# Issuing a kernel's DRAM stores from ScalarE instead of SyncE

## The chip, the cores and the metric

One core of a Trainium2 chip runs the program. The metric is the device time of one execution in microseconds (us). SP is the engine SyncE, which here does nothing but issue transfers; ACT is ScalarE, DVE VectorE, POOL GpSimd, PE TensorE.

## The reference

A one-layer hybrid encoder step, for a prompt of 2048 positions with 16 learned positions ahead of it, and for 8 short streams of 16 positions that have 256 cached positions each. All is float32.

```python
h = rmsnorm(x, norm_g)
q, k, v, z_a, f, B, C, h_c, z_c = split(h @ w_in)          # w_in: 1024 x 4104
logf = log_sigmoid(f + b_f);  c = cumsum(logf)              # per head
s = q.k / 8 + c_q - c_k, causal                             # 8 heads of 64
o = softmax(s) @ v * silu(z_a)
u = C * h_c;  y = B * conv3(u) * silu(z_c)                  # causal, width 3
x = x + concat(o, y) @ w_out
return rmsnorm(x, final_g), k, v, logf, last rows of u      # prompt and streams
```

## The kernel before

Float32 products are made of three float32r products: each operand is split into a high part (a ScalarE cast) and a low part (a VectorE subtraction), hence names that end in `h` and `l`.

The work comes in two token groups (1280 positions, then the rest). For each group the tokens are normalised and transposed (`hh`, `hl`), then the projections run: `keys`, `queries`, `gates` and `values` for four pairs of heads, later `conv` for four blocks of channels. Each projection fetches 128 columns of `w_in` (`raw`, 512 KB, issued from ScalarE), splits them (`wh`, `wl`) and runs 24 products into a PSUM tile `ps`, of which there are two. ScalarE or VectorE takes the result out into `kf`, `eh`, `el`, `sv`, `vv` or `st`, and it is stored to DRAM: keys to `kh_d` and `kl_d`, queries to `qh_d` and `ql_d`, gates to `gz_d`, values to `v_d`, convolution results to `cat_d`; outputs of the reference go to `out_dram`. `eh` and `el` have one buffer each (`EB = 1`), `kf` and `st` have two or fewer, so the next tile of that name waits until the store has landed.

Attention takes these back from DRAM: per head `ka`, `kb` and `vb`, per unit of 256 queries `qa`, `qb` and `gz`, and the running sums `c_d` in rows of 1 KB. A unit makes scores (`sp`, `s`), an exponential on ScalarE, transposes (`tp`), the split `ph` (ScalarE) and `pl` (VectorE), products with `vb` into `o`, and a store of the gated result to `cat_d`. Attention and projections are woven on TensorE. At the end the output stage loads 128 columns of positions from `cat_d` (`cr`), splits them (`ch`, `cl`), multiplies by `w_out`, adds `x`, normalises (`oxt`) and stores `y`, tile by tile.

The order of the work is fixed when the program is built. `Times` keeps a running clock for each engine; `weave` picks the next TensorE work by it, and every instruction of the other engines, transfers too, gets a key from the same clock, by which `settle` sorts each engine's queue. All engines but TensorE then go through their queue in that order. A transfer is an entry in the queue of the engine that issues it: it waits there for its data, for the room it writes to, and for one of eight completion counters (DMAHW0 to DMAHW7 in the program), which go round over the transfers of all queues; what stands behind it waits too.

Before the change every transfer but the 59 loads of `raw` goes through `Step.dma`:

```python
    def dma(self, out, in_):
        ...
        return self.nc.sync.dma_start(out=out, in_=in_)
```

Of the kernel before, what the change touches and what calls it, by code (L numbers as in the profile page):

```python
# [18 lines left out]
DRAM = bass.MemoryType.DRAM  # L19
# [48 lines left out]
class Times:  # L68
# [85 lines left out]
    def note(self, queue, op, a, k):  # L154
        k = dict(k)
        if op == "matmul":
            k.update(zip(("out", "lhsT", "rhs"), a))
        elif a:
            k.update(zip(("out", "in_"), a))
        writes = [k[x] for x in ("out", "accum_out") if k.get(x) is not None]  # L160
        if not writes:
            return
        reads = [self.region(v) for x, v in k.items() if isinstance(v, bass.AP) and x not in ("out", "accum_out")]
        cost_of, writes = writes[0], [self.region(w) for w in writes]
        ready = max(self.free(reads, False, queue), self.free(writes, True, queue))
        if op == "dma_start":
            size, run = 4.0, min(4.0 * self.run(k["out"]), 4.0 * self.run(k["in_"]))
            for x in cost_of.shape:
                size *= x
            size = max(size * (2 if run < 512 else 1) / 360.0, 0.4375 * size / run)  # L170
            self.key = self.place(queue, ready, 50.0) + self.LATENCY
            t = self.place("dge", self.key - self.LATENCY, 450.0 if cost_of.shape[0] == P else 650.0)
            t = self.place("dma", t + DMA_START, size)
            if queue == "sync":
                self.key = t - size
            t += DMA_LATENCY
        else:
            t = self.place(queue, ready, self.cost(queue, op, cost_of, k)) + self.LATENCY
            self.key = t
        for regions, wrote in ((reads, False), (writes, True)):  # L180
            for name, lo, hi in regions:
                if wrote and name not in self.begun:
                    self.begun[name] = t
                old = self.seen.setdefault(name, [])
                if len(old) > 100:
                    old[:] = [x for x in old if x[2] > self.pe - 40000.0]
                old.append((lo, hi, t, wrote, queue))
                self.used[name] = max(self.used.get(name, 0.0), t)
        return t
# [125 lines left out]
class Step:  # L315
# [7 lines left out]
    def dma(self, out, in_):  # L323

        if out.dtype == F32R:
            out = out.bitcast(F32)
        if in_.dtype == F32R:
            in_ = in_.bitcast(F32)
        return self.nc.sync.dma_start(out=out, in_=in_)

    def open(self, ctx, name, side=None, space=None):
        k = {}
# [47 lines left out]
    def load_constants(self, pool):  # L380
        nc, dma = self.nc, self.dma
        mraw = pool.tile([P, P], F32, name="mraw")
        dma(out=mraw, in_=self.cst[:, C_MASK:C_MASK + P])
        nc.vector.tensor_copy(out=self.mask, in_=mraw)
        for i in range(3):
            dma(out=self.cw[:, :, i], in_=self.conv_w[0, i].rearrange("(c p) -> p c", p=P))

        nc.vector.tensor_scalar(out=self.cw, in0=self.cw, scalar1=0.5, scalar2=None, op0=ALU.mult)
# [22 lines left out]
    def normalise(self, ph, xp, bufs, beside=()):  # L411
# [7 lines left out]
        def prepare():  # L419
            i, (pos, rows, ct, col) = todo.pop(0)  # L420
            xt = xp.tile([P, D], F32, name="xt", bufs=bufs)
            if pos == 0:
                dma(out=xt[:NMETA], in_=self.meta_tokens)
                dma(out=xt[NMETA:], in_=self.x_p[:P - NMETA])
            else:
                dma(out=xt[:rows], in_=self.x_s if pos == NPOS else self.x_p[pos - NMETA:pos - NMETA + rows])
            if pos == p0:
                dma(out=g_bc, in_=self.norm_g[0].partition_broadcast(P))
            if beside:
                beside.pop(0)()  # L430
            sq = xp.tile([P, D], BF16, name="sq")
            ss = xp.tile([P, 1], F32, name="ss", bufs=4)
            nc.scalar.activation(out=sq[:rows], in_=xt[:rows], func=AF.Square, accum_out=ss[:rows])
            self.rsqrt(ss[:rows])
            nc.vector.scalar_tensor_tensor(out=xt[:rows], in0=xt[:rows], scalar=ss[:rows, 0:1], in1=g_bc[:rows],
                                           op0=ALU.mult, op1=ALU.mult)
            ahead.append((xt, rows, ct, col, i))
# [834 lines left out]
    def load_out(self, pool, chunks, freed=()):  # L1272
# [3 lines left out]
        for c, n in chunks:  # L1276
# [8 lines left out]
            for a in range(2):  # L1285
                self.dma(out=self.o_hl[c, n][a], in_=self.o_d[a, :, c, cols])
            if c % PACE == PACE - 1:
                yield self.when(*self.o_hl[c, n])
# [256 lines left out]
WEARLY = 5  # L1545
EARLY = lambda e, a, b: [lambda: None, lambda: (e(a), e(b))]
PACE = 2
HI_ACT = 4
KFB = 2
GTN = 2  # L1550
# [69 lines left out]
```

## Time and profile before

| | us |
|---|---|
| three runs | 1741.93, 1729.77, 1734.06 |
| median | 1734.06 |
| the profiled execution | 1732.57 |
| its span, first to last instruction | 1730.8 |
| TensorE busy in it | 1578.8 |
| VectorE busy | 881.1 |
| ScalarE busy | 629.2 |
| GpSimd busy | 232.9 |

The rows quoted further down are from that one execution; times in them count from its first instruction. Busy time leaves out the issuing of transfers. All rows carry line L278, the helper that records every instruction, so that groups are told apart by tile.

### The profile page before, as it was taken

To read this page: it belongs to the slowest core of one execution; us is meant where nothing else is said; L and a number is where in the kernel's file an instruction comes from. 1 tells how busy PE (TensorE), PEld (TensorE's weight loads), DVE (VectorE), ACT (ScalarE), POOL (GpSimd) and SP (SyncE) were. 2 spreads that over 40 slices of the span, in tenths; PEclk is the share of its full clock that TensorE was granted. 3 is DMA by queue.
4 is the path that set the end of the run, shared out by engine and by line. 5 is a ranking of instruction groups with operands and counts; after the bars stand their busy time and mean duration, and the time that the engine had idled before them with its cause. 6 is when DMAs were issued, how large, how long until landed. Compare 5 with 4: busy or idle time off the path is not lost.

```text
span 1730.8 us, 27628 instructions
## 1 busy us (share of the span) xinstructions
PE 1578.8 (91%) x10311; PEld 1462.5 (84%) x10311; DVE 881.1 (51%) x2276; ACT 629.2 (36%) x1196; POOL 232.9 (13%) x320
## 2 busy tenths in 40 slices
PE   4977899989889899989995789999999999979998
PEld 4877889989889888989984779989889889968876
DVE  4424566526657566624321547667667657313443
ACT  4323445415435242421110435445545445312111
POOL 2200112100001120121020001000110101112222
PEclk9988999989999999999997889999999999989999
DMA  6454544364542386432136444446533413254443
GB/s 165 161 138 107 136 111 120 99 162 112 138 104 65 108 287 216 131 94 50 42 80 130 110 108 118 120 101 160 129 77 76 104 41 72 64 191 158 130 125 122
DMA packets 222241, 206.03 MB, mean 119 GB/s; under 512 B 26036, under 2 KB 196060, under 8 KB 220444
## 3 DMA queue, kind: packets, MB, share of 16 engines
q1 hardware_dynamic: 160748, 173.34, 34.0%
q10 hardware_dynamic: 61360, 30.94, 10.2%
q8 instruction: 81, 1.33, 0.3%
q14 instruction: 52, 0.43, 0.1%
HBM read 137.28 MB, written 66.93 MB: 118 GB/s over the span
## 4 chain that ended last, share of the span: by engine, by line
PE 59%; DMA 22%; DVE 5%; SPq 4%; issue 3%; ACT 3%; POOL 2%; ACTq 0%; POOLq 0%; DVEq 0%
PE ps L278 33%; PE sp L278 9%; PE o L278 9%; PE tp L278 7%; DMA raw<-in_w_in_dram 4%; SPq L278 4%; DMA cr<-cat_d 4%; DVE oxt L278 2%; DMA vb<-v_d 2%; PE tr L278 2%; DMA qh_d<-eh 1%; DMA qb<-ql_d 1%; DMA kb<-kh_d 1%; DMA gz_d<-kf 1%; DMA sqk_d<-el 1%
## 5 line engine op out<-in xcount | busy, mean ns | idle before, releaser
L278 PE MATMUL ps<-hh,wh 128*128 128x256 f32 (+2 forms) x1568 | 502.7, 321 | 23.6 <-DVE el L278 22.8
L278 PE MATMUL ps<-hl,wh 128*128 128x256 f32 (+2 forms) x1568 | 486.3, 310 | 0.0
L278 PE MATMUL ps<-hh,wl 128*128 128x256 f32 (+2 forms) x1568 | 486.0, 310 | 0.0
L278 PEld LDWEIGHTS ps<-hh,wh 128*128 128x128 f32 x1568 | 302.8, 193 | 34.1 <-DVE el L278 23.9
L278 PEld LDWEIGHTS ps<-hl,wh 128*128 128x128 f32 x1568 | 302.5, 193 | 1.8
L278 PEld LDWEIGHTS ps<-hh,wl 128*128 128x128 f32 x1568 | 301.5, 192 | 0.0
L278 DVE TENSOR_TENSOR pl<-tp,ph 128x512 fp32r<-128x512 f32 (+2 forms) x360 | 199.3, 564 | 121.3 <-ACT ph L278 117.7
L278 ACT CAST ph<-tp 128x512 fp32r<-128x512 f32 (+2 forms) x360 | 171.7, 486 | 224.4 <-PE tp L278 204.6
L278 DVE TENSOR_SCALAR_CACHE_REDUCE s<-sp 128x384 f32<-128x384 f32 (+3 forms) x360 | 211.4, 598 | 50.4 <-PE sp L278 48.8
L278 ACT ACTIVATE s<-s,nm 128x128 f32<-128x128 f32 (+16 forms) x136 | 170.5, 1254 | 84.4 <-DVE nm L278 81.9
L278 PE MATMUL tp<-ident,s 128*128 128x128 f32 (+1 forms) x1224 | 196.4, 272 | 5.0 <-DVE pl L278 5.0
L278 PE MATMUL o<-ph,vb 128*128 128x256 f32 (+4 forms) x584 | 169.8, 310 | 16.5 <-DMA vb<-v_d 11.4
L278 PEld LDWEIGHTS tp<-ident,s 128*128 128x128 f32 (+1 forms) x1224 | 148.5, 142 | 29.1 <-issue 20.9
L278 PE MATMUL sp<-kb,qb 68*128 68x384 f32 (+3 forms) x360 | 144.7, 402 | 24.2 <-DMA qb<-ql_d 20.5
L278 PE MATMUL o<-pl,vb 128*128 128x256 f32 (+4 forms) x584 | 151.2, 285 | 2.0 <-DVE pl L278 1.9
L278 POOL TENSOR_TENSOR gz<-gz,otmp 64x256 f32<-64x256 f32 (+1 forms) x64 | 47.1, 737 | 702.2 <-DVE otmp L278 629.5
L278 PE MATMUL sp<-ka,qa 128*128 128x384 f32 (+3 forms) x360 | 133.7, 371 | 0.0
L278 PEld LDWEIGHTS o<-ph,vb 128*128 128x128 f32 (+1 forms) x584 | 111.7, 191 | 23.9 <-DMA vb<-v_d 12.0
L278 PE MATMUL ps<-o,ch 128*128 128x512 f32 x374 | 118.9, 399 | 11.1 <-ACT ch L278 8.9
L278 PEld LDWEIGHTS o<-pl,vb 128*128 128x128 f32 (+1 forms) x584 | 112.4, 192 | 3.3 <-DVE pl L278 2.6
L278 PEld LDWEIGHTS ps<-o,ch 128*128 128x128 f32 x374 | 70.6, 191 | 29.7 <-ACT ch L278 9.3
L278 DVE TENSOR_TENSOR wl<-raw,wh 128x1024 fp32r<-128x1024 f32 x56 | 69.3, 1238 | 47.5 <-ACT wh L278 47.3
(193 smaller groups left out, 2080.5 us busy)
## 6 DMA issues: line engine op xcount, KB each, us to landing
raw<-in_w_in_dram ACTq DMA_DIRECT2D x59, 512.0 KB
cr<-cat_d SPq DMA_DIRECT2D x17, 512.0 KB
v_d<-vv SPq DMA_DIRECT2D x32, 256.0 KB
vb<-v_d SPq DMA_DIRECT2D x8, 1024.0 KB
oxt<-in_x_prompt_dram SPq DMA_DIRECT2D x16, 512.0 KB
out_dram<-oxt SPq DMA_DIRECT2D x16, 512.0 KB
xt<-in_x_prompt_dram SPq DMA_DIRECT2D x15, 512.0 KB
qa<-qh_d SPq DMA_DIRECT2D x112, 64.0 KB
```

What stands on the lines that cost most here:

```text
L278: r = f(*a, **k)
```

## The change

`Step.dma` picks the engine by where the transfer writes: to DRAM, ScalarE; else SP as before. The loads of `raw` were on ScalarE already. In `Times` the price of an issue by GpSimd is changed as well, but no transfer is issued from there.

```diff
-            self.key = self.place(queue, ready, 50.0) + self.LATENCY
+            self.key = self.place(queue, ready, 1000.0 if queue == "gpsimd" else 50.0) + self.LATENCY
...
-        return self.nc.sync.dma_start(out=out, in_=in_)
+        return getattr(self.nc, STORES if out.space == DRAM else "sync").dma_start(out=out, in_=in_)
...
+STORES = "scalar"
```

The built program has 1129 transfers, of which 422 write to DRAM. The order of the other engines moves a little too, since the clock that sorts them sees other queues.

ScalarE's queue before, where the second token group's last queries and first gates are projected (`eh`: high part of the queries, `kf`: gates, `wh<-raw`: weight split; in brackets what a row waits for, PE and DVE for their results, DMAHW for a completion counter):

```order
L278 ACTIVATE eh<-ps 128x272 [waits DMAHW2_49,PE_49]
L278 ACTIVATE kf<-ps 128x256 [waits PE_49] x2
L278 CAST wh<-raw 128x1024 [waits DMAHW5_49,PE_49]
L278 DMA raw<-in_w_in_dram 128x8x128 [waits DMAHW4_49,DVE_49]
L278 ACTIVATE kf<-ps 128x272 [waits DMAHW6_49,PE_49]
```

The same place of ScalarE's queue after the change:

```order
L278 ACTIVATE eh<-ps 128x272 [waits DMAHW7_49,PE_49]
L278 DMA qh_d_92<-eh 128x272 [waits Activation_49]
L278 DMA raw<-in_w_in_dram 128x8x128 [waits DMAHW1_49,DVE_49]
L278 ACTIVATE kf<-ps 128x256 [waits PE_49]
L278 DMA ql_d_96<-el 128x272 [waits DMAHW3_49,DVE_49]
L278 DMA gz_d_111<-kf 128x256 [waits DMAHW5_49,DVE_49]
L278 ACTIVATE kf<-ps 128x256 [waits PE_49]
L278 CAST wh<-raw 128x1024 [waits DMAHW1_49,PE_49]
L278 DMA raw<-in_w_in_dram 128x8x128 [waits DMAHW3_49,DVE_49]
L278 DMA gz_d_111<-kf 128x256 [waits DMAHW4_49]
```

Four stores now stand between the evacuations of `ps`, each with waits of its own.

SP's queue before, at the same place (`ka` and `kb`: keys of a head, `qa` and `qb`: queries of a unit):

```order
L278 DMA ka_9632<-kh_d_100 64x2064
L278 DMA qh_d_92<-eh 128x256
L278 DMA ql_d_96<-el 128x256
L278 DMA ka_9632<-kl_d_104 64x2064
L278 DMA qh_d_92<-eh 128x272
L278 DMA ql_d_96<-el 128x272
L278 DMA kb_9634<-kh_d_100 64x2064
L278 DMA ka_9633<-kh_d_100 64x2064
L278 DMA ka_9633<-kl_d_104 64x2064
L278 DMA kb_9635<-kh_d_100 64x2064
L278 DMA qa_9637<-qh_d_92 64x256 x2
```

SP's queue there after the change:

```order
L278 DMA ka_9632<-kh_d_100 64x2064
L278 DMA ka_9632<-kl_d_104 64x2064
L278 DMA kb_9634<-kh_d_100 64x2064
L278 DMA ka_9633<-kh_d_100 64x2064
L278 DMA ka_9633<-kl_d_104 64x2064
L278 DMA kb_9635<-kh_d_100 64x2064
L278 DMA qa_9637<-qh_d_92 64x256 x2
L278 DMA qb_9639<-ql_d_96 64x256
```

The stores between the loads are gone, and the six loads of two heads follow each other.

## Rows read from the trace of the kernel before

**Rows 1.** The page: busy time, share of the span and instructions.

```profile
PE 1578.8 (91%) x10311; PEld 1462.5 (84%) x10311; DVE 881.1 (51%) x2276; ACT 629.2 (36%) x1196; POOL 232.9 (13%) x320
```

**Rows 2.** Stretches of the span; columns in the first row.

```profile
core 0: us, PE busy (x) PEld busy (x) DVE busy (x) ACT busy (x) POOL busy (x), PEclk, DMA share, GB/s
...
890.00:1030.00 140.00, 100.93 (x695) 93.41 (x694) 52.63 (x137) 42.27 (x78) 12.74 (x10) 0.85 0.54 117
1030.00:1260.00 230.00, 229.57 (x1650) 209.10 (x1650) 151.84 (x430) 117.37 (x215) 19.30 (x28) 0.99 0.47 121
...
1560.00:1705.00 145.00, 142.94 (x615) 114.78 (x614) 57.49 (x50) 26.21 (x37) 37.68 (x25) 1.00 0.44 141
```

**Rows 3.** TensorE's waits: us in total, times, longest us.

```profile
PE ps L278 <- DVE el L278: 22.8, 4, 10.1
PE sp L278 <- DMA qb<-ql_d: 20.5, 6, 10.2
PE tr L278 <- ACT kf L278: 17.9, 5, 10.6
...
PE o L278 <- DMA vb<-v_d: 11.4, 4, 8.8
```

**Rows 4.** The waits of SP's queue.

```profile
SPq L278 <- DVE oxt L278: 129.0, 16, 17.1
SPq L278 <- POOL kf L278: 120.0, 27, 15.0
SPq L278 <- POOL gz L278: 119.2, 37, 27.6
```

**Rows 5.** ScalarE's issues of `raw`: duration ns min/median/max, first and last start.

```profile
L278 ACTq DMA_DIRECT2D raw<-in_w_in_dram x59: 373/374/448, 31.3 to 1489.2; - x59
```

**Rows 6.** ScalarE in order of time, four stretches: start, us, operation, idle before.

```profile
238.25 0.59 ACT L278 CAST ph<-tp 128x512 fp32r<-128x512 f32 x1 [0.77 <-PE tp L278]
240.73 0.37 ACTq L278 DMA_DIRECT2D raw<-in_w_in_dram  x1
...
905.49 0.51 ACT L278 COPY st<-tr 128x256 f32<-128x256 f32 x2
906.88 0.43 ACTq L278 DMA_DIRECT2D raw<-in_w_in_dram  x1
...
935.22 1.05 ACT L278 CAST wh<-raw 128x1024 fp32r<-128x1024 f32 x1 [3.83 <-DMA raw<-in_w_in_dram]
946.48 0.38 ACTq L278 DMA_DIRECT2D raw<-in_w_in_dram  x1
959.87 0.40 ACT L278 ACTIVATE kf<-ps 128x272 f32<-128x272 f32 x1 [23.60 <-DMA gz_d<-kf]
...
1212.53 0.73 ACT L278 CAST ph<-tp 128x272 fp32r<-128x272 f32 x2
1215.60 0.39 ACTq L278 DMA_DIRECT2D raw<-in_w_in_dram  x1
```

**Rows 7.** SP's queue in order of time around 930 to 950 us.

```profile
931.62 0.59 SPq L278 DMA_DIRECT2D kb<-kh_d  x1
932.25 3.35 SPq L278 DMA_DIRECT2D qa<-qh_d  x2
...
939.00 2.91 SPq L278 DMA_DIRECT2D qa<-qh_d  x2
```

**Rows 8.** The chain of waits: start of a transfer's issue, us until it landed.

```profile
345.30 2.08 DMA kl_d<-el
...
911.91 10.02 DMA qh_d<-eh
...
931.62 14.59 DMA kb<-kh_d
...
947.58 12.21 DMA gz_d<-kf
```

**Rows 9.** The chain of waits in the output stage, one turn.

```profile
1616.95 4.25 DMA cr<-cat_d
...
1624.31 3.44 DVE oxt L278
1627.75 0.02 issue
1627.77 0.34 SPq L278
```

## Prediction

> **What bounds the kernel now.** The totals come first [rows 1]: TensorE is busy for 1578.8 of 1730.8 us, so 152 us is all that it is idle, and a change that moves transfers can save little more than a part of that. ScalarE, which gets the stores, is busy for 629.2 us; it has room on average. The stretches show that the average hides two kinds of stage [rows 2]. From 1030 to 1260 us TensorE works 229.57 of 230 us with a granted clock of 0.99 (the 2.4 GHz level but for short drops); from 890 to 1030, where the second token group's keys, queries and gates are projected while attention starts, it works 100.93 of 140 us at 0.85. In the output stage (1560 to 1705) it works 142.94 of 145. So whatever SP is waiting for in the output stage costs TensorE 2 us at most, and the stage that can gain is the one around 890 to 1030.
>
> Next, what TensorE waits for [rows 3]: `el` (22.8 us in 4 waits), the query tiles `qb` (20.5 us in 6), `kf` (17.9 us in 5), `vb` (11.4 us). `el`, `eh` and `kf` are tiles that a projection may only refill when their store has landed; `qb` and `vb` are loads. Then SP's own waits [rows 4]: it stands 129.0, 120.0 and 119.2 us at stores whose data DVE or POOL has not finished. Those look large, but SP does nothing else, and only what stands behind such a store is late.
>
> **What moves.** 422 transfers of 1129 write to DRAM. All leave SP (1070 transfers before, 648 after) and join the 59 weight loads on ScalarE (481 after). The number of transfers and their bytes stay. Three prices are to be found: the time to issue, the time that ScalarE stands at a store that may not start yet, and what SP gains.
>
> *Issue.* A weight load takes ScalarE's queue 374 ns [rows 5], whatever it moves; 422 x 0.374 = 158 us. ScalarE is idle for 1730.8 - 629.2 = 1102 us [rows 1], so I take 0 on the path. The cover is thinnest from 1030 to 1260, where ScalarE already works 117.37 of 230 us [rows 2] and its copies stand between the transposes and the products. About 100 of the stores lie behind 890 us and before 1260; all of them exposed would be 37 us, the upper end.
>
> *Standing at a completion counter.* Every transfer of both queues takes one of eight completion counters in turn, and may not be issued before the transfer that had it last has landed. On SP such a wait stops only transfers. On ScalarE it stops every copy and exponential behind it. After the change 200 stores and 33 weight loads on ScalarE wait in this way for a load of SP; before, 29 weight loads did. At the place shown ahead, the store `ql_d<-el` shares its counter (DMAHW3) with a load of `qa` on SP, and two evacuations, a weight split and a weight load are queued behind it; TensorE waits for all four. What one such wait costs is in the trace of before: of the 59 weight loads on ScalarE four were released by a counter, after 1.9 us (240.73, the instruction before ended at 238.84), 10.2 us (946.48 after 936.27), 1.3 us and 2.3 us (1215.60 after 1213.26) [rows 6], 15.7 us together. The long one is a pile-up: SP had six loads of whole heads in flight, then query loads [rows 7], and the weight load's counter belonged to one of those. Per transfer in ScalarE's queue that is 15.7 / 59 = 0.27 us, and 422 x 0.27 = 112 us. The short waits, 5.5 us, hide behind the two PSUM buffers of each kind; a wait of 10 us does not, since TensorE runs at most two groups ahead. 10.2 / 15.7 = 65% reaches TensorE: **+73 us**. Ends: 0 if the counters come free before the stores reach them, 112 if all of it counts.
>
> *Standing at data.* The order of ScalarE puts a store where the kernel's own clock says that its data is done. The other 55 weight loads, placed by the same rule, start a mean of 0.7 us after the end of the instruction ahead of them (39 us in all; the one at 906.88 came 0.88 us behind the end of `st` at 906.00, [rows 6]); mostly ScalarE had nothing to do then. I take 0; 422 x 0.7 = 295 us, a quarter of it on TensorE's path, gives 75 us as the upper end.
>
> *What SP gives back.* In 890 to 1030 the loads of heads and queries stood behind stores on SP, and the gate store `gz_d<-kf` (issued 947.58, 12.21 us to land, [rows 8]) stood behind them; ScalarE's next `kf` waited until 959.87 after 23.60 us of idleness [rows 6]. The two TensorE waits that follow, 10.2 us for `qb` and 10.6 us for `kf` [rows 3], could go: 20.8 us. With them goes some of the clock: 100.93 us of work at 0.85 is 86.7 us at 0.99 [rows 2], 14 us. **-35 us** if all of it goes. Lower end of the sum: also the other five waits for `qb`, 20.5 - 10.2 = 10.3 us, so -45.
>
> *Clock of new stalls.* By the same stage, 39 us of idleness came with 14 us of slower work, 0.36 us each. Net new idleness of 73 - 35 = 38 us costs **+14 us**.
>
> *Output stage.* The loop of this stage, seen in the chain, is load 4.25 us, normalisation 3.44 us, store issue on SP, next load [rows 9], and it repeats with TensorE at work throughout [rows 2]. The store leaves SP and the load starts 0.34 us sooner; at most 2 us, taken as 0.
>
> Sum against the profiled execution (1732.57 us, of which the span is 1730.8; 1.5 us below the median of 1734.06): 1732.6 + 73 - 35 + 14 = 1784.6, with the median's 1.5 us some 1786. **I forecast 1785 us**, its own range 1752 to 1890.
>
> A rule of the Trainium skill on the gain: its page "DMA: Bandwidth & Descriptors", section "Issuing engines are not separate DMA queues", says that transfers started by different engines run on the same DMA engines, and that spreading them saves only the issuing time. The trace agrees as far as it goes: a store on SP and a weight load on ScalarE, two queues, slowed each other down (10.02 us for the store of `qh_d` issued 5 us after the load at 906.88, against 2.08 us for a store at 345.30 [rows 6, 8]). By the rule alone the -35 would be near 0 and the sum about 1833.
>
> **The rivals.**
>
> *Faster: the loads get out.* SP without stores issues a head's loads as soon as the keys have landed. They are done before ScalarE's stores come to the same counters, so nothing stands on ScalarE. For it: SP's waits [rows 4] are the largest in the trace, and 55 of 59 weight loads waited for no counter. Against it: stores keep their place between bursts of loads, and in the pile-up the loads themselves take the time (the last head load of the burst took 14.59 us to land, [rows 8]). It decides if the mean counter wait on ScalarE is under 35 / 422 / 0.65 = 0.13 us, half of what weight loads showed. Time: 1732.6 - 45 = 1688.
>
> *Hidden.* ScalarE's 158 us of issuing and its waits all fall into its 1102 us of idleness and SP's waits cost nothing before, so nothing moves: 1735, give or take 15. For it: TensorE at 229.57 of 230 us beside a ScalarE that is half busy [rows 2].
>
> *Slower through the ring.* Stores now follow weight loads in one queue. A store alone landed in 2.08 us, two beside a weight load in 10.02 and 12.21 [rows 8]. If they now wait for the whole load ahead of them more often, the waits for `el` double: 22.8 us and 0.36 of that for the clock, 31 us; with a gain of 5 from SP, 1758. The page named above, section "Queues, rings and completion order", says that a DMA engine takes packets from its rows in turn, by which a row of its own protects a store and the weight load's row does not. The two stores beside weight loads were on a row of their own and took 10 and 12 us all the same, so the trace speaks against that protection.
>
> That the change does not do what it says is excluded: the built program has the 422 stores on ScalarE.
>
> **How the numbers follow.** ScalarE held up, 1785: 0.55, since the mechanism is in the trace and the program has it on 233 transfers where it was on 29. Ring, 1758: 0.10. Hidden, 1735: 0.17. Faster, 1688: 0.18. A measurement here tells 1% from nothing, 17 us. Faster by over 1%: 0.18; within: 0.19 (hidden, and the edge of the ring); slower: 0.63. The range goes from 1700 (most of the faster case left out at its far end) to 1890: the sum with all of 112 on the path and both upper ends of issue and data would be 1732.6 + 112 + 37 + 75 - 35 = 1922; all three at once is unlikely.
>
> **What would show it.** In the profile after: ScalarE's queue entries (issues) grow by 422 with about 0.37 us each; idle gaps of 5 to 15 us on ScalarE just behind a store of `ql_d`, `gz_d`, `cat_d` or `out_dram<-st`, ended by the landing of a load (`qa`, `qb`, `kb`, `vb`); TensorE's waits for ScalarE's copies (`ph`, `kf`, `eh`, and DVE's `pl` and `el` behind them) grow well past the 40.7 us that `el` and `kf` make now [rows 3]; its waits for `qb` shrink; the output stage stays within 2 us. The forecast is wrong if ScalarE's gaps behind stores stay under 2 us (then hidden or faster), or if ScalarE's waits for data alone, not counters, make up the loss.

## The result and the profile after

The changed kernel takes 1746.96 us, the median of 11 runs (1740.55 to 1760.52); the kernel before, in 11 runs beside it, 1734.12 us. The ratio is 1.0082, with an interval of 1.0058 to 1.0106: slower by 13 us where 51 were forecast, inside the whole range (1700 to 1890) and just under the forecast's own (1752 to 1890). The profiled execution took 1746.78 us, its span 14.2 us more than that of before.

The page after, busy time and share of the span [rows 1]:

```profile
PE 1594.7 (91%) x10311; PEld 1474.3 (84%) x10311; DVE 879.7 (50%) x2276; ACT 633.0 (36%) x1196; POOL 235.5 (13%) x320
```

TensorE is busy 15.9 us longer for the same products, so it ran them at a lower clock: its busy time at the 1.2 GHz level rose from 88.7 to 117.8 us, and half of that rise, 14.6 us, is what the level of half the speed adds. Its idle time hardly moved (its waits sum to 143.8 us before, 142.9 after). The stretches after, to set beside [rows 2], and two short ones:

```profile
core 0: us, PE busy (x) PEld busy (x) DVE busy (x) ACT busy (x) POOL busy (x), PEclk, DMA share, GB/s
...
890.00:1030.00 140.00, 102.38 (x695) 95.31 (x693) 51.79 (x135) 42.57 (x77) 13.63 (x12) 0.87 0.52 120
1030.00:1260.00 230.00, 224.16 (x1479) 199.31 (x1477) 132.67 (x379) 106.18 (x197) 15.32 (x23) 0.90 0.43 111
...
1560.00:1705.00 145.00, 143.50 (x615) 115.19 (x616) 56.95 (x52) 28.39 (x40) 39.95 (x26) 1.00 0.46 148
...
1080.00:1100.00 20.00, 18.69 (x87) 14.60 (x86) 6.40 (x16) 5.35 (x15) 0.45 (x1) 0.66 0.33 77
...
1240.00:1260.00 20.00, 20.00 (x97) 17.00 (x96) 7.52 (x23) 7.60 (x16) 3.13 (x2) 0.66 0.09 23
```

The stage that was to gain, 890 to 1030, stands as it was. The stage behind it, which had 0.99 of the clock, now has 0.90, in two dips (the last two rows). What TensorE waits for after [rows 3]:

```profile
PE ps L278 <- DVE el L278: 39.5, 6, 12.5
PE tr L278 <- ACT kf L278: 15.1, 5, 11.0
PE o L278 <- DVE otmp L278: 14.2, 4, 6.0
...
PE o L278 <- ACT ph L278: 6.7, 4, 4.5
PE tp L278 <- DVE pl L278: 6.4, 7, 2.9
...
PE sp L278 <- DMA kn<-in_cache_k_dram: 4.4, 1, 4.4
...
PE o L278 <- DMA vb<-v_d: 2.9, 1, 2.9
```

The waits for `qb` are gone and all waits for transfers together fell from 45.7 to 9.0 us; the waits for `el`, `otmp`, `ph` and other work of ScalarE and VectorE rose by the same 36 us. ScalarE's engine in time ahead of the second dip:

```profile
1222.70 0.19 ACT L278 ACTIVATION_READ_ACCUMULATOR s<-s,nm 128x1 f32 x1
1226.62 0.39 ACTq L278 DMA_DIRECT2D raw<-in_w_in_dram  x1
1227.06 0.67 ACT L278 CAST ph<-tp 128x272 fp32r<-128x272 f32 x2 [4.17 <-DMA kb<-c_d]
```

Here a weight load stood 3.7 us at its counter until a load of SP had landed, with a cast of `ph` behind it; TensorE then waited 2.9 us for `pl`, and from 1229.8 it ran at 1.2 GHz for 23.9 us. This is the forecast mechanism, but it is rare: summed over the trace (the time from the end of the entry ahead to the issue, where the counter came last), ScalarE stands 7.9 us at counters in front of 8 stores and 4.4 us in front of 2 weight loads, where the forecast had 112. At stores whose data VectorE or GpSimd had not finished it stands 186 us, 61 of them in the output stage.

### The profile page after: what moved, and what is told of

It is laid out like the page before. It is cut to its first block, busy times and chain, and to the rows that moved or that the text cites. A ratio compares the mean times of both kernels' runs of the same rounds, so it can differ in the third digit from the quotient of the medians.

```text
span 1745.0 us, 27558 instructions
## 1 busy us (share of the span) xinstructions
PE 1594.7 (91%) x10311; PEld 1474.3 (84%) x10311; DVE 879.7 (50%) x2276; ACT 633.0 (36%) x1196; POOL 235.5 (13%) x320
## 4 chain that ended last, share of the span: by engine, by line
PE 44%; DMA 7%; ACT 1%; DVE 1%; issue 1%; ACTq 1%; POOL 0%; SPq 0%; POOLq 0%; DVEq 0%
PE ps L278 28%; PE o L278 6%; PE tp L278 5%; PE sp L278 5%; DMA raw<-in_w_in_dram 1%; DMA ql_d<-el 1%; DMA gz_d<-kf 1%; DMA o<-o_d 1%; DMA kh_d<-eh 1%; DMA vb<-v_d 1%; ACTq L278 1%; PE tr L278 1%; DMA kb<-c_d 0%; ACT s L278 0%; DMA cat_d<-kf 0%
## 5 line engine op out<-in xcount | busy, mean ns | idle before, releaser
L278 PE MATMUL ps<-hh,wh 128*128 128x256 f32 (+2 forms) x1568 | 507.7, 324 | 40.1 <-DVE el L278 39.5
L278 PEld LDWEIGHTS ps<-hl,wh 128*128 128x128 f32 x1568 | 306.1, 195 | 1.6
L278 PE MATMUL tp<-ident,s 128*128 128x128 f32 (+1 forms) x1224 | 204.7, 279 | 11.0 <-DVE pl L278 6.4
L278 PE MATMUL o<-ph,vb 128*128 128x256 f32 (+4 forms) x584 | 175.9, 319 | 23.8 <-DVE otmp L278 14.2
L278 PEld LDWEIGHTS tp<-ident,s 128*128 128x128 f32 (+1 forms) x1224 | 152.2, 145 | 40.7 <-issue 23.7
L278 PE MATMUL o<-pl,vb 128*128 128x256 f32 (+4 forms) x584 | 156.7, 293 | 1.7 <-DVE pl L278 1.7
L278 PEld LDWEIGHTS o<-ph,vb 128*128 128x128 f32 (+1 forms) x584 | 115.5, 198 | 32.1 <-DVE otmp L278 12.1
L278 PEld LDWEIGHTS o<-pl,vb 128*128 128x128 f32 (+1 forms) x584 | 116.9, 200 | 3.7 <-DVE pl L278 2.9
L278 ACT CAST wh<-raw 128x1024 fp32r<-128x1024 f32 x56 | 58.7, 1048 | 101.9 <-PE ps L278 66.9
```

The source lines that it names most:

```text
L278: r = f(*a, **k)
```

## The experiments

The theories that the expectations name. T1: ScalarE's standing at unfinished data is the loss. T2: the order that the clock makes with stores on ScalarE is worse in itself. T3: stores behind weight loads in one queue. T4: the time to issue. Later ones are told where they come in.

### First four: which stores, the order alone, the standing alone

ScalarE issues only the 108 stores whose data it makes itself (`sv`, `st`, `oh`, the high part of the queries), or only the 314 others:

```diff
-        return getattr(self.nc, STORES if out.space == DRAM else "sync").dma_start(out=out, in_=in_)
+        src, dst = (a.tensor.name.rsplit("_", 1)[0] for a in (in_, out))
+        made = src in ("sv", "st", "oh") or dst.startswith("qh_d")
+        on = "scalar" if out.space == DRAM and made else "sync"      # or: not made
+        return getattr(self.nc, on).dma_start(out=out, in_=in_)
```

> ScalarE issues only the 108 stores whose tile it wrote itself (sv, st, oh and the high part of the queries); the other 314 stay on SP. Theory 1 (ScalarE stands at stores whose data VectorE or GpSimd has yet to finish): hardly any standing, a quarter of what SP's loads gain, so 1720 to 1735 us. Theory 2 (the new order that the kernel's clock makes is worse in itself): no forecast from it, the order is a third one. Theory 3 (a store behind a weight load in one queue lands late): the sv, st and qh_d stores are such, so 1738 to 1745. Theory 4 (issuing time on ScalarE): a quarter of the loss, 1737.

> The reverse: ScalarE issues the 314 stores whose tile VectorE or GpSimd wrote, SP the 108 that ScalarE wrote. Theory 1: all of the standing with part of the gain, 1745 to 1765 us. Theory 3: between, 1740 to 1746. Theory 4: three quarters of the loss, 1744.

Measured: 1735.12 us, 0.9973 (0.9947 to 0.9999), and 1745.63 us, 1.0048 (1.0021 to 1.0076). Each has an order of its own, and the runs further down show what that alone can do, so neither tells a theory from another.

The order alone: SP issues every store, but the clock counts stores as ScalarE's, so that TensorE, VectorE and GpSimd have the changed kernel's order row for row.

```diff
-            t = self.times.note(self.name, op, a, k)
+            as_ = "scalar" if self.name == "sync" and k["out"].space == DRAM else self.name
+            t = self.times.note(as_, op, a, k)
```

> The order of TensorE, VectorE and GpSimd is that of the changed kernel, row for row, but SP issues the stores. Theory 2: 1745 to 1750 us as in the changed kernel. Theories 1, 3 and 4: no loss on ScalarE and no gain on SP, so 1728 to 1740, with TensorE's waits for transfers near the 46 us of before.

Measured: 1756.37 us, 1.0105 (1.0069 to 1.0142). The whole loss of the changed kernel is there without one store on ScalarE. At this order the move itself is worth 1.0082 / 1.0105 = 0.998, within its uncertainty of 0.4% nothing. What it exchanges is seen in TensorE's waits of this run:

```profile
PE ps L278 <- DVE el L278: 26.0, 3, 10.9
PE o L278 <- DMA vb<-v_d: 24.9, 10, 10.8
PE sp L278 <- DMA qb<-ql_d: 22.6, 3, 15.6
PE sp L278 <- DMA qb<-c_d: 16.9, 4, 8.6
```

The waits for `vb` and `qb`, 64 us, are 2.9 us in the changed kernel; `el` is 39.5 there instead of 26.0. In the two profiles, moving the stores takes TensorE's waits from 158.8 to 142.9 us and adds 8.3 us to its busy time (1586.4 to 1594.7), which is clock: of the time that waits gave back, half went there.

The standing alone: all transfers on SP, but ahead of each store ScalarE copies one column of the tile that is stored, and so waits for its data.

```diff
+        if out.space == DRAM:
+            part = in_[(slice(None),) + (0,) * (len(in_.shape) - 2) + (slice(0, 1),)]
+            self.nc.scalar.copy(out=self.touch[:in_.shape[0]], in_=part)
         return self.nc.sync.dma_start(out=out, in_=in_)
```

> All transfers stay on SP as before, but ScalarE copies one column of the tile of each of the 422 stores (about 0.2 us each), at the place where the store would stand, and so waits for the data. Theory 1: the loss without the gain, TensorE's waits for other engines up by 30 to 40 us and 1765 to 1785 us. Theories 3 and 4 (the queue or the issue itself): 1734 to 1742.

Measured: 1734.36 us, 0.9975 (0.995 to 1.0). 422 copies that wait for unfinished data cost nothing that shows, against T1. The waits were really there: ScalarE sat idle some 220 us right ahead of the copies, 62 of it at `oxt` in the output stage. The order was made anew here too, which can move a time by 1% (further down), so this speaks against T1 and does not exclude it.

### The queue alone, and other orders

The complement of the order alone: the clock counts stores as SP's, so the rows of TensorE, VectorE and GpSimd stand as before, one by one; ScalarE issues the stores, each where the clock would have SP ask for it.

```diff
+            self.asked = self.key
...
-            t = self.times.note(self.name, op, a, k)
+            store = op == "dma_start" and k["out"].space == DRAM
+            t = self.times.note("sync" if store else self.name, op, a, k)
...
-                todo.append((self.times.key, len(todo), r.ins))
+                todo.append((self.times.asked if store else self.times.key, len(todo), r.ins))
```

> The rows of TensorE, VectorE and GpSimd stand as before, one by one; only the 422 stores are issued from ScalarE, each at the place where the kernel's clock, which still counts them as SP's, has its data done. Theory T2 (the order that the clock makes with stores on ScalarE costs about 1%, the queue itself gains): the order's loss is gone and the queue's gain stays, so 0.990 to 0.998 of before, about 1722 to 1736 us. Rival T1b (the standing of ScalarE at stores costs about 1% in any order): 1.005 to 1.012. Rival T5 (each order is tuned for its own queues, so that the queue's gain is seen only in the order after): 0.998 to 1.005.

Measured: 1755.09 us, 1.0115 (1.0082 to 1.0149). T2's gain of the queue doesn't come; at the order of before the move costs 20 us. TensorE's waits, in which the loads are gone as in the changed kernel (15.5 us of waits for transfers):

```profile
PE ps L279 <- DVE el L279: 42.0, 5, 19.5
...
PE tp L279 <- DVE pl L279: 12.1, 7, 7.0
PE tp L279 <- ACT s L279: 11.7, 11, 6.2
```

Two things are in these rows. The longest wait for `el` ends at 945; ScalarE issued the store `ql_d<-el` at 922.63, 2 us behind a weight load (920.66), and VectorE, which writes `el` next, waited for it, while SP, with no stores between its loads, had begun six loads of 516 KB from 921.55 on (SP's first two and last of them, then VectorE, start, us, idle before):

```profile
921.55 0.51 SPq L279 DMA_DIRECT2D ka<-kh_d  x1
922.15 3.33 SPq L279 DMA_DIRECT2D ka<-kl_d  x1
...
935.89 0.51 SPq L279 DMA_DIRECT2D kb<-kh_d  x1
```

```profile
944.95 0.42 DVE L279 SCALAR_TENSOR_TENSOR el<-ps,eh 128x256 fp32r<-128x256 f32 x1 [22.35 <-DMA ql_d<-el]
```

What moved in those 22 us is in the packets: queue `q10` is ScalarE's (a weight load goes in pieces of 512 bytes), `q1` SP's. First the window 922 to 932, then 933 to 943:

```profile
q10 hardware_dynamic: 859, 0.44, 43.2%
```

```profile
q1 hardware_dynamic: 264, 1.80, 82.2%
q10 hardware_dynamic: 382, 0.31, 20.0%
```

In the first window the weight load alone moves packets: `ql_d<-el` stands behind it in its queue, and SP's first five loads have not moved a packet either. From 933 the store moves, beside those loads, until 942. So some 11 of the 22 us lie behind the weight load, and some 9 beside the loads that went ahead. The first part is no matter of ScalarE's queue: in the kernel before, SP's store `qh_d<-eh`, issued at 911.91, 5 us behind the weight load of 906.88, moved its first packet at 918.4, and from 912 to 918 only the weight load's queue moves (538 packets, 43.7%). It isn't always so (from 926.6 to 933.7 in that kernel a weight load's packets and SP's ran side by side), and what decides was not found. New with the move is the second part.

And here ScalarE does stand at counters, 57.9 us in front of 17 stores and 2.5 us at a weight load; the longest stand, in ScalarE's order of time:

```profile
1226.98 0.39 ACT L279 CAST ph<-tp 128x272 fp32r<-128x272 f32 x1
1236.07 0.35 ACTq L279 DMA_DIRECT2D gz_d<-kf  x1
1236.46 0.39 ACT L279 CAST ph<-tp 128x272 fp32r<-128x272 f32 x1 [9.10 <-DMA kb<-kh_d]
```

A store of a finished gate stood 8.7 us until the load of `kb` on SP, which had its counter, landed.

Is the changed kernel's order bad for a reason, or is it just another order? The clock lets stores of SP to one DRAM tensor overlap, and chains those of ScalarE; one run takes that away in the changed kernel. Four change only the price of an issue in the clock, 50 ns, to 100 or 20, in the kernel before and in the changed one.

```diff
-                if end > t and not (q == queue == "sync" and wrote and writes) and ...
+                if end > t and not (q == queue and wrote and writes and (q == "sync" or "_d" in name)) and ...
```

```diff
-            self.key = self.place(queue, ready, 50.0) + self.LATENCY
+            self.key = self.place(queue, ready, 100.0) + self.LATENCY      # or 20.0
```

> The changed kernel, but the kernel's clock lets stores on ScalarE to one DRAM tensor run beside each other, as it did for stores on SP; in the changed kernel it chains each to the landing of the one before. T2 with this chain as the reason of the worse order: 0.992 to 1.001 of before. T2 with another reason (any new order has some such loss): 1.004 to 1.012, as the changed kernel's 1.008.

> The kernel before, all stores on SP; only the clock's price of an issue is 100 ns in place of 50, by which TensorE's order comes out anew. If any change of the order costs up to 1% by chance (T6: order noise): 1.003 to 1.012. If only the order that the changed queues make is bad (T2 proper): 0.997 to 1.003.

> The kernel before with 20 ns in place of 50 as the clock's price of an issue, a second new order that has nothing to do with the change. T6 (order noise): outside 0.997 to 1.003, on either side. T2 proper: 0.997 to 1.003.

> The changed kernel with 100 ns in place of 50 as the clock's price of an issue, so that all orders come out anew. T6 (a new order by itself moves the time by up to 1%, and the change's loss is such a throw): anywhere from 0.998 to 1.014 of before, and not the changed kernel's 1.008. T9 (issuing stores from ScalarE costs about 1% in any order that is made for it): 1.006 to 1.012.

> The changed kernel with 20 ns as the clock's price of an issue, one more order. T6: anywhere from 0.998 to 1.014 of before. T9: 1.006 to 1.012. Together with the run at 100 ns: if both lie above the kernel before at the same prices (1.010 at 100 ns, 1.006 at 20 ns), the change itself costs something beside the throw; if below, it gains.

Measured, the chained stores set free: 1764.65 us, 1.0157 (1.0117 to 1.0198), so the chain is not the reason; this lies above what either theory expected. Other prices without the change: 1.0104 (1.0068 to 1.014) at 100 and 1.0057 (1.003 to 1.0085) at 20. With it: 1.0077 (1.0053 to 1.0101) at 100 and 0.9974 (0.9953 to 0.9995) at 20. A price that has nothing to do with the change moves the kernel before by as much as the change did. Price by price the change is worth 1.0082 at 50, a loss beyond its 0.24%; 1.0077 / 1.0104 = 0.997 at 100, within the uncertainty of 0.4% nothing; and 0.9974 / 1.0057 = 0.992 at 20, a gain beyond 0.35%. T9, about 1% in any order, falls with the 0.9974. T6 is left: the sign is that of the order that happens to come out. It is not proven: 1.0077 is the value of the changed kernel that T6 had left out, and the two kernels of a price differ in order as well as in queue.

What does not depend on the throw is seen when the profiles of all orders stand side by side (sums from each profile: TensorE's idle time that ends with a transfer, with all else, ScalarE's standing at counters, and the time at 1.2 GHz, of which some 2 us in each row lie behind the last instruction):

| stores on | order of | ratio | for transfers | other idle | at counters | at 1.2 GHz |
|---|---|---|---|---|---|---|
| SP | before | 1 | 45.7 | 98.1 | 15.7 | 139.6 |
| SP | the changed kernel | 1.0105 | 74.6 | 84.2 | 8.9 | 155.5 |
| SP | price 100 | 1.0104 | 47.4 | 110.5 | 15.5 | 166.4 |
| SP | price 20 | 1.0057 | 53.2 | 105.2 | 18.4 | 156.7 |
| ScalarE | the changed kernel | 1.0082 | 9.0 | 133.9 | 12.3 | 158.8 |
| ScalarE | price 100 | 1.0077 | 7.4 | 142.3 | 42.7 | 175.5 |
| ScalarE | price 20 | 0.9974 | 6.3 | 135.9 | 33.4 | 142.1 |
| ScalarE | stores set free | 1.0157 | 12.0 | 138.7 | 62.7 | 151.4 |
| ScalarE | before | 1.0115 | 15.5 | 147.6 | 60.4 | 140.9 |

With stores on ScalarE the waits for loads all but vanish in every order, and waits for ScalarE's and VectorE's work take their place in every order.

### At the order of before: which stores, and where

From here on TensorE, VectorE and GpSimd keep the order of before, so that the rows of TensorE are the same in each, and one kernel's time at a row can be set against another's. First the 112 stores of split keys and queries against the other 310, T7 against T8:

```diff
+        eh_el = out.tensor.name[:4] in ("kh_d", "kl_d", "qh_d", "ql_d")
+        on = "scalar" if out.space == DRAM and not eh_el else "sync"      # or: and eh_el
+        return getattr(self.nc, on).dma_start(out=out, in_=in_)
```

> TensorE, VectorE and GpSimd in the order of before, row for row. The 112 stores of the split keys and queries (kh_d, kl_d, qh_d, ql_d, whose landing frees eh and el) stay on SP between the loads; the other 310 are issued from ScalarE. T7 (the loss of the version with all stores on ScalarE comes from loads that get ahead and crowd the stores that free el): 0.992 to 1.001 of before. T8 (it comes from ScalarE standing at counters and data and issuing, whatever the store): 1.006 to 1.011.

> The complement, in the same order of the three engines: ScalarE issues only the 112 stores of the split keys and queries, SP the other 310. T7: 1.006 to 1.013 of before, with long waits for el around 945 us. T8: 1.001 to 1.005, by the share of the stores.

Measured: the 310 alone 1732.17 us, 0.996 (0.9941 to 0.998); the 112 alone 1741.41 us, 1.0013 (0.9995 to 1.0031). The first is as T7 expected it, the second as T8 did; neither theory foretold both, and neither part is the 1.0115 of both moved together. TensorE's waits with the 112:

```profile
PE ps L279 <- DVE el L279: 40.7, 4, 18.0
...
PE tr L279 <- ACT kf L279: 9.5, 4, 3.8
...
PE sp L279 <- DMA qb<-ql_d: 6.7, 3, 3.1
```

`el` costs 18 us more than before, as T7 has it (22.0 with the 310), but `qb` and `kf` cost 22 us less [rows 3]; by the row of TensorE that stood at 1217 before, this kernel is only 2.6 us behind. The 310 win and lose: they are 16.5 us ahead of before at the row that stood at 1034.9, and 3.2 us behind at the one of 1209.9. That stage gave the next question, with T10 and T11: the stores as far as 1030 us, those behind it, and all but six of the 310, gate stores behind that place, one of which stood 8.5 us (T12, T13). `late` is true from the work that TensorE reaches at 1030 us on.

```diff
+        late = self.nc.pe > 822000.0
+        on = "scalar" if out.space == DRAM and not eh_el and not late else "sync"
+        # or: not eh_el and late
+        # or: not eh_el and not (late and name.startswith("gz_d"))
```

> TensorE, VectorE and GpSimd in the order of before. ScalarE issues 228 stores: those that are not of the split keys and queries, and only as far as the place that TensorE reaches at 1030 us; all behind it stay on SP. T10 (the price of stores on ScalarE is paid from 1035 to 1215 us, where TensorE had no idle time and ScalarE the least room: the version with all 310 such stores lost some 20 us there): 0.981 to 0.989 of before, about 1710 to 1720 us. Rival T11 (what is won or lost in one stage is given back in the next, since loads and projections run ahead of each other): 0.993 to 0.999, as the version with all 310.

> The complement: the 82 stores of that kind behind that place on ScalarE, everything else on SP, in the order of before. T10: 1.008 to 1.013 of before, all of it lost between 1035 and 1215 us. T11: 0.998 to 1.004.

> The version with the 310 stores on ScalarE (0.996 of before), but the six gate stores (gz_d) behind that place stay on SP. One of them stood 8.5 us on ScalarE at the counter of a 516 KB load of keys. T12 (that stand is a large part of the loss in the stage): 0.988 to 0.993. Rival T13 (the loss is the sum of many small stands and issues, or another store takes the counter and stands in its place): 0.994 to 0.999.

Measured: early ones 1722.53 us, 0.9914 (0.9893 to 0.9934); late ones 1748.06 us, 1.0049 (1.0023 to 1.0074); the two together make 0.9963, which is what all 310 showed. Both lie between T10 and T11. All but the six: 1716.62 us, 0.9887 (0.9862 to 0.9912), so T12: six stores of 310 cost 0.996 / 0.9887, 0.73% or 12.7 us, give or take 0.3%, and without them the other late stores cost nothing that shows. How, is in ScalarE's timeline with the 310:

```profile
1202.89 0.39 ACT L279 CAST ph<-tp 128x272 fp32r<-128x272 f32 x1
1211.76 0.35 ACTq L279 DMA_DIRECT2D gz_d<-kf  x1
1212.15 0.39 ACT L279 CAST ph<-tp 128x272 fp32r<-128x272 f32 x1 [8.88 <-DMA kb<-kh_d]
```

in the chain of waits there (the load of `kb` took 12.23 us, and the store was issued when it had landed),

```profile
1199.46 12.23 DMA kb<-kh_d
```

and in TensorE's waits of 1190 to 1216:

```profile
PE tp L279 <- DVE pl L279: 6.8, 1, 6.8
```

The gate was ready. Behind its store stood the cast `ph`, behind that `pl`, behind that TensorE: 6.8 of 8.5 us arrive. Another of the six stood 1.9 us, until 1128.96, and cost TensorE 0.2 us. A third cost more by its landing than by its issue: it kept its `kf` buffer for 10.4 us, and ScalarE's next gate waited for it, with the weight split `wh` and the `pl` of the next products behind (the chain, and ScalarE):

```profile
1122.73 10.39 DMA gz_d<-kf
```

```profile
1133.19 0.40 ACT L279 ACTIVATE kf<-ps 128x272 f32<-128x272 f32 x1 [1.43 <-DMA gz_d<-kf]
```

TensorE waited 1.2 us at 1137, and from 1139.1 it ran at 1.2 GHz for 17.1 us. The stretch behind it, with the 310 and then without the six:

```profile
1135.00:1155.00 20.00, 18.85 (x82) 15.02 (x81) 8.04 (x19) 5.73 (x16) 0.00 (x0) 0.60 0.24 53
1035.00:1215.00 180.00, 168.86 (x1171) 151.61 (x1171) 106.99 (x307) 84.88 (x154) 10.63 (x16) 0.94 0.47 120
```

```profile
1135.00:1155.00 20.00, 19.43 (x133) 16.62 (x132) 10.03 (x30) 7.93 (x19) 0.76 (x1) 1.00 0.37 88
1035.00:1215.00 180.00, 177.84 (x1283) 159.74 (x1281) 113.83 (x322) 92.29 (x171) 12.20 (x17) 1.00 0.50 127
```

82 matmuls in those 20 us against 133 (not all of them the same ones). Row against row the six stores cost 2 us before 1137, 6 in the slow stretch up to 1154, 2 as far as 1202 and 8 at and just behind the long stand; 15.7 of these are left at the end of the two spans.

Last, whether these stands are also in the 1.15% of all 422: all stores early, all but the six, and the 310 without any gate store.

```diff
+        on = "scalar" if out.space == DRAM and not late else "sync"
+        # or: not (late and name.startswith("gz_d"))
+        # or: not eh_el and not name.startswith("gz_d")
```

> All stores as far as that place on ScalarE (316, those of the split keys and queries too), those behind it on SP, in the order of before. T10: the version with all 422 had lost 10 us by that place and 18 us in the stage behind it, so 1.004 to 1.008. Rival T7 (the stores that free el, crowded by the loads, are the larger part): 1.008 to 1.013.

> The order of before; all stores on ScalarE but the same six late gate stores, which stay on SP. With all 422 (1.0115 of before) one of them stood 8.7 us at the counter of a load of keys, another 3.5 us. T12 (a stand of that length there is worth some 0.7%): 1.002 to 1.007. Rival T7 (with all stores gone from SP the loss is the crowding of the stores that free el, so six gate stores don't matter): 1.009 to 1.013.

> The order of before; ScalarE issues 282 stores: neither those of the split keys and queries nor any gate store. Against the version that left only the six late gate stores on SP (0.989 of before) the stands of 4.9 us at 237 us and 3.9 us at 928 us, both of gate stores at counters, go. T12: 0.984 to 0.988. Rival T13 (the counters stop the next entry in their place): 0.988 to 0.993.

Measured: all early 1741.98 us, 1.0019 (1.0003 to 1.0035), a little better than both expected. All but the six 1744.87 us, 1.0033 (1.0011 to 1.0055): the same six stores are worth 0.8% here too. No gate store at all 1718.25 us, 0.9878 (0.9837 to 0.9919): within the uncertainty the same as without the six, so what the stands that are left cost stays open between T12 and T13.

The 88 early stores of split keys and queries cost 1.0019 / 0.9914, 1.1% (give or take 0.26%), once the other early stores have left SP as well, and all 112 of them 0.1% when they go alone. In the run with all early, ScalarE stands 35.4 us at counters in front of stores from 100 to 520, against 14.7 without the 88; two of the stands are `ql_d<-el` at the counters of loads of `qa`, 10.1 and 9.0 us. The second, ScalarE in time and TensorE's wait from 445 to 475:

```profile
456.28 0.19 ACT L279 ACTIVATION_READ_ACCUMULATOR s<-s,nm 128x1 f32 x1
465.42 0.33 ACTq L279 DMA_DIRECT2D ql_d<-el  x1
465.79 0.36 ACT L279 COPY otmp<-o 64x256 f32<-64x256 f32 x1 [9.32 <-DMA qa<-qh_d]
```

```profile
PE o L279 <- DVE otmp L279: 8.2, 1, 8.2
```

What these stands cost is less than that wait suggests. Row against row, the kernel with the 88 is 5 us behind the one without them both before and after the first stand (208.6 to 218.7), so its 10.1 us reached no row; a stand of 6.3 us of `cat_d<-gz` near 245 puts it 9 us behind. It is 7 to 8 us behind ahead of the second stand, 16 to 18 just behind it and 12 soon after. At 890 it is 10 us behind; it loses 18 more up to 957, where `el` waits (24.2 us in 900 to 1030 against 12.4), and of these it has made up 15 by 974. It is 18 us behind at 1027 and 19 at the end. So about half of the 1.1% arises before 900 and the rest from there to 1030; how much belongs to each stand and how much to `el` stays open, and no run left these two stores alone on SP.

## Why the prediction was wrong

*The failed step: "Standing at a completion counter", +73 us.* It took the weight loads' 0.27 us for each of 422 stores. In the changed kernel counters hold ScalarE for 12.3 us in all its 481 transfers, 0.03 us each. The mechanism was right and was shown by itself: finished stores stood 8.5, 8.7 and 9.0 us at a counter of a load of SP, and six gate stores cost 12.7 us, of it 7 to 9 at and behind the longest stand. The size was wrong because standing is no rate. A few long stands make it, and which stores meet them hangs on the order: 12.3, 33.4, 42.7, 60.4 and 62.7 us in five orders with all stores on ScalarE. Even the largest is little more than half of 112. The prediction's point of decision, 0.13 us per transfer, was no better: 60.4 / 481 = 0.126 at the order of before went with a loss of 1.15%. The share that reaches TensorE, forecast as 65%, is no rate either: 6.8 of 8.5 us, 8.2 of 9.0, none of 10.1.

*A term that was missing: the order.* The change moves the clock's order on every engine, which was named ("moves a little too") and priced at nothing. With all stores on SP this order costs 1.05% by itself, and other prices of an issue cost 1.04% and 0.57%. That is as large as the whole result. The 13 us measured can't be put down to ScalarE's queue alone: at the changed kernel's order the queue costs nothing, at that of before 20 us. The parts don't add up either: the order costs 1.0105 and the queue 1.0115, and both together 1.0082. Why the order of before is better than the others was not found.

*What SP gives back, -35.* Confirmed for the waits: 45.7 to 9.0 us for transfers, of which 20.5 were `qb`; 30 to 66 us less than with stores on SP at the same order or price. The 14 us of clock in 890 to 1030 didn't come (0.85 to 0.87), since the waits for `el` and `kf` stayed there. The 10.6 us for `kf` were no gift of SP's loads to begin with, as the prediction read them. The gate store issued at 947.58 stood behind the weight load issued at 946.48; in the window 948 to 957 only that load's queue moves bulk:

```profile
q10 hardware_dynamic: 840, 0.43, 43.6%
```

After the change a gate store stands behind a weight load again, and TensorE waits 11.0 us for `kf` instead of 10.6. The "store alone" of 2.08 us, which the prediction sets beside these, had two other stores in flight with it, but no bulk load. The rule of the Trainium skill's page "DMA: Bandwidth & Descriptors", section "Issuing engines are not separate DMA queues", by which this term would be near 0, is not borne out by TensorE's waits for transfers, which fell by 36.7 us; in time, at this order, next to nothing of it is left. That transfers started by different engines share what carries them, as it says, agrees with the window 933 to 943 above, in which SP's queue took 82.2% and ScalarE's 20.0% of the DMA engines' time.

*Issue, 0.* The median issue of a store takes 0.35 us, near the forecast 0.374, but the 422 together take 202 us, 0.48 each: 25 of them hold ScalarE for 0.8 to 4.0 us, and 23 of these began within 6 us behind a weight load on the same queue. Of the late stores, 76 on ScalarE (0.9887) and none (0.9914) don't differ by more than the uncertainty, so 0 holds there. In the changed kernel it does not hold everywhere. ScalarE around 441 and around 1082:

```profile
441.53 3.93 ACTq L278 DMA_DIRECT2D out_dram<-st  x2
445.50 1.58 ACTq L278 DMA_DIRECT2D sqk_d<-el  x1
447.12 0.48 ACT L278 CAST ph<-tp 128x384 fp32r<-128x384 f32 x1 [5.97 <-issue]
```

```profile
1081.94 1.12 ACTq L278 DMA_DIRECT2D kh_d<-eh  x1
1083.10 0.39 ACT L278 CAST ph<-tp 128x272 fp32r<-128x272 f32 x1 [1.99 <-PE tp L278]
```

At 441 three issues behind a weight load (441.04) keep the cast `ph` waiting, and TensorE waits 4.5 us for it, the longest of its waits for `ph`. At 1082 the transposes for the cast were done at 1082.46, but the issue held ScalarE until 1083.1; TensorE waits 0.8 and 0.5 us, and the first dip of the clock follows. What the long issues cost in all was not measured by a run.

*Standing at data, 0.* 186 us of it in the changed kernel. The same pair says 0 for the late stores, and 422 waits of that kind without a store (0.9975, in an order of their own) speak for it.

*Clock of new stalls, +14.* Near what was measured (15.9 us more of busy time) and for another reason, so by luck: idle time did not grow. Two dips make most of it, 20.5 us from 1086.5 behind the long issue, and 23.9 us from 1229.8 behind a weight load at its counter; 44 of the 117.8 us at 1.2 GHz are in them, and the stage had 7 before.

*Output stage, 0.* TensorE works 143.50 of 145 us, against 142.94.

*The rivals.* Hidden came nearest in time (1735), but by a balance and not by cover. Faster is what a part of the move becomes once the longest stand is gone, 0.9887. The ring, 1758, foresaw the near-doubled waits for `el`, 22.8 to 39.5 us. In the run looked at, half of the longest of these is a store behind a weight load, as the ring has it, but stores on SP met that before the change as well; the other half is SP's loads. T3, stores behind weight loads, had no run of its own.

## What to carry to other kernels

A store on a compute engine costs what stands behind it. Look at which completion counter or whose data it will wait for at the place where that engine's work is on the path, and move only stores that won't wait there: at the order of before, 304 of these 422 gain 1.1%, 422 lose 1.15%, and six of them decide 0.7%. An issue close behind a large load in the same queue can itself hold the engine for some us. Where a model sorts the program, any edit throws a new order; measure that throw first, with an edit that means nothing, and hold the order while parts are compared. Stores between loads in one queue also pace the loads: taken out, the loads go ahead and share the DMA engines with the stores that free a buffer (some 9 of the 22 us of the wait shown).

## What the runs showed of the hardware

TensorE's clock fell to its 1.2 GHz level behind short waits, in the three places looked at: from 1139.1 with the 310 stores, behind a wait of 1.2 us; after the change from 1086.5, behind waits of 0.8 and 0.5 us, and from 1229.8, behind one of 2.9 us. It stayed there for 17.1, 20.5 and 23.9 us, although TensorE was busy all that time. A wait of 1.2 us was so followed by some 6 us lost in the stretch behind it.

In three windows, while a weight load of 512 KB in pieces of 512 bytes moved at 44 to 50 GB/s (its packets 43% of the DMA engines' time), bulk transfers that were issued behind it, in either queue, moved no packet: 922 to 932 with all stores on ScalarE, 912 to 918 and 948 to 957 before. At another place (926.6 to 933.7 before) both queues ran side by side. A store of a split key landed in 2.08 us beside two other stores [rows 8]; one of split queries kept its buffer for some 22 us behind a weight load and then beside loads of whole heads.

An issue on ScalarE, at a median of 0.35 us, took 0.8 to 4.0 us in 25 of 422 stores, 23 of which began within 6 us behind a weight load in the same queue.
